# A decoder layer whose compression weights move to buffers of their own, in halves, with the instruction order planned anew

## The chip, the cores and the metric

The kernel runs on one core of a Trainium2 chip. The metric is device time in microseconds (us) of one execution; lower is better. One execution was also taken by the hardware profiler, and all rows below come from it. The engines are TensorE (PE in the rows; PEld is its weight load), VectorE (DVE), ScalarE (ACT), GpSimd (POOL) and SyncE (SP), which issues most transfers.

## The reference, cut to what matters

One layer on 512 tokens of width 1024. A single projection of the normalised input feeds three groups, whose gated outputs are concatenated and projected back:

```python
xn = _rmsnorm(h, g_in[l])
proj = xn @ w_in[l]
...
# A: sparse attention. Its compressed branch first makes 31 blocks of 32 tokens:
def compress(a, pos_emb, w1, w2):
    chunks = a.reshape(B, S // CMP_STRIDE, CMP_STRIDE, G, Dh)
    blocks = jnp.concatenate([chunks[:, r:r + n_cmp] for r in range(R)], axis=2)
    blocks = blocks + pos_emb[:, None, :]
    flat = blocks.transpose(0, 1, 3, 2, 4).reshape(B, n_cmp, G, CMP_LEN * Dh)
    return jax.nn.silu(flat @ w1) @ w2
kc = compress(k_c, pos_k, w1_k, w2_k)
vc = compress(v_c, pos_v, w1_v, w2_v)
...
# B: a chunked state-space scan; its decay matrix is exp of differences of a running sum
decay_in = jnp.exp(jnp.where(causal, a_cs[..., :, None] - a_cs[..., None, :], -jnp.inf))
y_diag = jnp.einsum('bcgels,bcsgep->bclgep', cb[:, :, :, None] * decay_in, xdt)
...
# C: attention into 256 memory tokens
kv = _rmsnorm(mem, g_mem) @ w_mem_kv
...
h = h + jnp.concatenate([o_a, o_b, o_c], axis=-1) @ w_out[l]
return _rmsnorm(h, g_final)
```

## The kernel before, in words

**Arithmetic.** Most products are made of two-part numbers. A weight chunk of 512 KB lands as 128x1024 floats in a tile `wst`; a copy rounds it to `whi` (on ACT or DVE), and a subtraction makes the rest `wlo` (on DVE or POOL). TensorE then multiplies high by high, high by low and low by high. The function `chunk` (line 488) does this for all weights.

**Buffers.** `wst` has two slots (WS), `whi` and `wlo` have three each (WH). A slot of `wst` is free when copy and subtraction are done; a slot of `whi`/`wlo` is free when TensorE has used it. All weights share them: the 24 tiles of the input projection (`in_wd`, product `pj`, 24 matmuls a chunk), the memory keys and values (`in_wmk`, `in_wmv`, product `pjm`), the value projection (`in_wv`, `pjv`), the compression's first layer (`in_w1k`, `in_w1v`, product `ph`, 8 matmuls a chunk, 4 chunks each for keys and values, line 608), the output projection (`pop`, `po`).

**Order.** Nothing is issued as the code runs. A class `Program` records every operation; `plan` (line 258) then plays all five engines forward with a table of costs (`cost`, line 222) and picks for each free engine the ready operation with the lowest number plus a hand-given offset (`BIAS`, and `LEAN` where two engines can do it). That is why every instruction has line 373 in the profile: rows are told apart by tile names. The stages are recorded in the order of the string `ORDER` (line 40): `z0`, `z1` the gate of the scan with the input's norm, `x0` to `x7` the scan's inputs (a convolution in `cacc`, its result `xst` or `bct`, transposed through `pxs`), `m0`, `m1` the memory's norm (`mf`, then `mh`, `ml`), `ki`, `vi` the compression's inputs (`cin`, `ft`, `fs`), `k`, `v` one chunk of the compression each, `mk`, `mv` memory keys and values, `s` one piece of the scan. Behind them come the attention, woven with the remaining projections, and the output projection.

**The scan's decay matrix `R`** (line 1127), one per chunk of 128 tokens, is filled by two transfers: a mask (`R<-in_mt`, on SP's queue), onto which POOL's queue adds the rows of the running sum (`R<-a_rows`). ACT then takes 8 exponentials, DVE multiplies by `pcb`, and TensorE uses it in 8 products `py`.

**Fillers.** TensorE starts with WARM products of zeros (`wps<-idle`) and has SPARE further ones (`wps<-xh`) after the transposes of the input (line 452).

**Tiles the change reuses.** `qst` (5 slots of 128x512) holds the scaled queries (line 720) and `pr` (4 slots) the attention's probabilities (line 797).

Of the kernel before, what the change touches and what calls it, by code (L numbers as in the profile page):

```python
# [42 lines left out]
WA, WX = 53.73, 123.88  # L43
BA, BS, BO = -31, 81, -25
BIAS = {("R", "activation"): 348, ("R", "dma_start"): -287, ("R", "tensor_tensor"): -67, ("a", "dma_start"): 21,
        ("ang", "tensor_copy"): -41, ("at", "activation"): 43, ("bct", "scalar_tensor_tensor"): -71,
        ("btok", "activation"): -227, ("cacc", "scalar_tensor_tensor"): 31, ("cin", "activation"): -1,
        ("cwh", "tensor_scalar"): 45, ("den", "activation"): 129, ("den", "reciprocal"): -233, ("den", "tensor_tensor"): 40,
        ("dout", "activation"): -81, ("dout", "tensor_tensor"): 228, ("dt", "scalar_tensor_tensor"): -45,
        ("dtd", "tensor_tensor"): -48, ("dtr", "tensor_copy"): -10, ("dw", "reciprocal"): 92,  # L50
        ("dw", "scalar_tensor_tensor"): 60, ("dw", "tensor_scalar"): -4, ("dw", "tensor_tensor"): -100,
        ("ea", "activation"): 50, ("eal", "activation"): 94, ("fs", "activation"): 60, ("ft", "tensor_tensor"): 52,
        ("gat", "scalar_tensor_tensor"): 205, ("gin", "dma_start"): -4, ("gps", "matmul"): 83, ("grow", "dma_start"): 2,
        ("gssd", "tensor_scalar"): -2, ("gxt", "scalar_tensor_tensor"): -13, ("idle", "memset"): -100,
        ("kc", "activation"): -112, ("kc", "tensor_tensor"): -52, ("kcs", "memset"): -96, ("kcs", "tensor_copy"): 30,
        ("kcs", "tensor_tensor"): -22, ("kk", "tensor_scalar"): -171, ("km", "activation"): -112, ("km", "tensor_tensor"): -8,
        ("kst0", "activation"): 4, ("kst0", "tensor_tensor"): -124, ("kst1", "tensor_tensor"): -50,
        ("ksw", "stream_shuffle"): 112, ("ksw", "tensor_tensor"): 30, ("lastb", "tensor_copy"): -257,
        ("mf", "tensor_tensor"): -100, ("mh", "activation"): 45, ("mhalf", "activation"): 5, ("mhalf", "memset"): -1,
        ("mhalf", "tensor_scalar"): -100, ("ml", "tensor_tensor"): 124, ("mt", "activation"): -32, ("mt", "dma_start"): 30,  # L60
        ("nacs", "tensor_scalar"): 8, ("o2", "activation"): -208, ("o2", "tensor_tensor"): -98,
        ("oa", "scalar_tensor_tensor"): -68, ("ob", "tensor_tensor"): 57, ("oh", "activation"): 40,
        ("oph", "activation"): 164, ("opl", "tensor_tensor"): 30, ("ot", "activation"): -44, ("pact", "transpose"): -410,
        ("pc", "activation"): 162, ("pc", "tensor_tensor"): 15, ("pcb", "matmul"): -114, ("pcs", "memset"): 243,
        ("pcs", "tensor_tensor"): -10, ("pcs_", "matmul"): -471, ("pjm", "matmul"): -11, ("pjv", "matmul"): -32,
        ("pjz", "matmul"): 105, ("pk", "matmul"): 20, ("po", "matmul"): 44, ("po2", "matmul"): 56, ("po3", "matmul"): 23,
        ("pop", "matmul"): 120, ("posi", "dma_start"): 25, ("pr", "activation"): -30, ("prev", "activation"): 30,
        ("prm", "dma_start"): 165, ("pt", "transpose"): 2, ("pth", "activation"): 405, ("ptl", "tensor_tensor"): 160,
        ("pturn", "transpose"): 96, ("pv", "matmul"): -51, ("pxs", "transpose"): 38, ("py", "matmul"): 234,
        ("py2", "matmul"): -213, ("pyt", "transpose"): 64, ("qr", "tensor_tensor"): -199, ("qst", "activation"): -34,  # L70
        ("qst", "scalar_tensor_tensor"): 429, ("rb", "matmul"): -12, ("rc", "tensor_scalar"): -200,
# [6 lines left out]
        ("vcs", "memset"): -100, ("vm", "activation"): 69, ("vm", "tensor_tensor"): 10, ("vst", "activation"): 30,  # L78
        ("vst", "tensor_tensor"): -15, ("whi", "activation"): 364, ("wlo", "tensor_tensor"): -4, ("wps", "matmul"): -83,
        ("wst", "dma_start"): -15, ("wst0", "dma_start"): -273, ("x", "scalar_tensor_tensor"): 224, ("x", "tensor_tensor"): 8,  # L80
        ("xdd", "tensor_tensor"): -95, ("xdt", "tensor_tensor"): -93, ("xh", "activation"): 96, ("xl", "tensor_tensor"): 150,
        ("xn", "activation"): 136, ("xnm", "reciprocal"): 156, ("xnm", "tensor_reduce"): -287, ("xnm", "tensor_scalar"): -8,
        ("xo", "matmul"): -230, ("xp", "tensor_tensor"): -15, ("xpt", "transpose"): -906, ("xqh", "activation"): 57,
        ("xql", "tensor_tensor"): 79, ("xs", "matmul"): -97, ("xst", "scalar_tensor_tensor"): 48,
        ("xstok", "activation"): -24, ("y", "tensor_tensor"): -192, ("yn", "tensor_scalar"): 85,
        ("yo", "tensor_tensor"): -204, ("z2", "scalar_tensor_tensor"): -64}
# [1387 lines left out]
```

## Time and profile before

| | us |
|---|---|
| three executions | 426.02, 427.02, 431.97 |
| median | 427.02 |
| profiled execution, whole | 426.92 |
| its span, first to last instruction | 425.1 |
| TensorE busy | 407.9 (96%) |
| VectorE busy | 327.4 (77%) |
| ScalarE busy | 217.3 (51%) |
| GpSimd busy | 185.9 (44%) |

Busy time counts a matmul from start to end; matmuls overlap, so two that follow each other without a wait start 0.23 us apart and last 0.4 us each. A wait shorter than that overlap doesn't show as idle time. In a timeline row, the bracket gives the idle time of the engine just before the row and what ended it.

### The profile page before, as it was taken

The numbers are of one execution on the slowest core, as the hardware profiler recorded it, in microseconds if no ns is written. First come the engines' busy times: TensorE is split into PE (matmuls) and PEld (weight loads), VectorE is DVE, ScalarE is ACT, GpSimd is POOL, SyncE is SP. The second block draws the span as 40 slices with busy tenths as digits, with TensorE's granted clock in tenths as the row PEclk, the third lists the DMA queues.
The fourth block names the chain that finished last, engine by engine and source line by source line (L and its number), as shares of the span: only waits on it lengthen the run. The fifth ranks groups of instructions, "written<-read, shape, count | busy, mean of one in ns | idle before, by whom it ended". The sixth has DMA issues, their size and how long they took to land.

```text
span 425.1 us, 6477 instructions
## 1 busy us (share of the span) xinstructions
PE 407.9 (96%) x2319; PEld 349.3 (82%) x2319; DVE 327.4 (77%) x678; ACT 217.3 (51%) x508; POOL 185.9 (44%) x127
## 2 busy tenths in 40 slices
PE   7999999979899999999999999999999999999992
PEld 4998899869788989988888878888787888788871
DVE  4879886687468769787978898897889878767665
ACT  5632355725385336525747366484667674270035
POOL 2552033457734948345553333323256282423142
PEclk9999999989999999999999999999999999999998
DMA  8954318222954534332120211141115103303105
GB/s 289 368 171 153 108 54 194 102 82 98 252 169 146 172 110 126 109 140 99 50 69 32 100 42 59 49 150 49 52 50 199 49 2 99 99 2 99 51 1 197
DMA packets 19572, 47.19 MB, mean 111 GB/s; under 512 B 1586, under 2 KB 8402, under 8 KB 19540
## 3 DMA queue, kind: packets, MB, share of 16 engines
q1 hardware_dynamic: 18816, 44.48, 31.3%
q0 software_dynamic: 576, 2.10, 2.7%
q8 instruction: 18, 0.29, 0.3%
q10 hardware_dynamic: 148, 0.20, 0.1%
q14 instruction: 14, 0.11, 0.1%
HBM read 44.66 MB, written 2.11 MB: 110 GB/s over the span
## 4 chain that ended last, share of the span: by engine, by line
PE 77%; ACT 6%; DVE 6%; DMA 6%; issue 2%; POOL 1%; SPq 0%; POOLq 0%; DVEq 0%; ACTq 0%
PE pj L373 31%; PE pop L373 9%; PE po L373 8%; PE sc L373 5%; PE pjz L373 4%; PE pt L373 4%; PE pjv L373 3%; PE pjm L373 3%; DMA R<-a_rows 2%; DMA wst<-in_wd 2%; PE xs L373 1%; DMA x<-in_x 1%; ACT whi L373 1%; PE xo L373 1%; PE py L373 1%
## 5 line engine op out<-in xcount | busy, mean ns | idle before, releaser
L373 POOL TENSOR_TENSOR wlo<-wst,whi 128x1024 fp32r<-128x1024 f32 (+1 forms) x32 | 76.3, 2389 | 106.0 <-ACT whi L373 60.8
L373 PE MATMUL pj<-xh,whi 128*128 128x512 f32 x224 | 90.7, 405 | 0.0
L373 PE MATMUL pj<-xh,wlo 128*128 128x512 f32 x224 | 90.0, 402 | 0.0
L373 PE MATMUL pj<-xl,whi 128*128 128x512 f32 x224 | 89.1, 398 | 0.0
L373 ACT ACTIVATE whi<-wst 128x1024 fp32r<-128x1024 f32 (+3 forms) x44 | 45.4, 1032 | 38.5 <-PE pj L373 8.6
L373 DVE TENSOR_TENSOR wlo<-wst,whi 128x1024 fp32r<-128x1024 f32 (+3 forms) x32 | 41.9, 1310 | 12.0 <-ACT whi L373 8.8
L373 PEld LDWEIGHTS pj<-xl,whi 128*128 128x128 f32 x224 | 42.6, 190 | 8.3
L373 PEld LDWEIGHTS pj<-xh,wlo 128*128 128x128 f32 x224 | 42.6, 190 | 7.5
L373 PEld LDWEIGHTS pj<-xh,whi 128*128 128x128 f32 x224 | 42.4, 189 | 7.4
L373 ACT ACTIVATE pr<-sc,nm 128x256 f32<-128x256 f32 (+3 forms) x64 | 33.1, 524 | 28.3 <-PE pt L373 16.5
L373 DVE CUSTOM_DVE_ANT_0 sc<-sc,cst 128x256 f32<-128x256 f32 (+3 forms) x64 | 30.9, 495 | 4.3 <-PE sc L373 4.0
L373 DVE TENSOR_TENSOR ptl<-pt,pth 128x512 fp32r<-128x512 f32 x40 | 27.0, 683 | 1.5 <-DVE pth L373 0.5
L373 PE MATMUL sc<-kst,qst 128*128 128x512 f32 (+2 forms) x96 | 27.4, 365 | 0.4 <-ACT pr L373 0.3
L373 PE MATMUL pt<-cst,pr 128*128 128x128 f32 x160 | 27.6, 273 | 0.0
L373 DVE CAST pth<-pt 128x512 fp32r<-128x512 f32 x30 | 20.3, 687 | 7.4 <-PE pt L373 6.9
L373 PE MATMUL pop<-whi,oph 128*128 128x512 f32 x64 | 25.8, 402 | 0.0
L373 PE MATMUL pop<-wlo,oph 128*128 128x512 f32 x64 | 25.4, 399 | 0.0
L373 PE MATMUL pop<-whi,opl 128*128 128x512 f32 x64 | 25.2, 396 | 0.0
L373 PEld LDWEIGHTS pt<-cst,pr 128*128 128x128 f32 x160 | 20.0, 140 | 3.8 <-issue 0.5
L373 PE MATMUL po<-pth,vst 128*128 128x256 f32 x80 | 22.4, 290 | 0.0
L373 PE MATMUL po<-ptl,vst 128*128 128x256 f32 x80 | 21.7, 287 | 0.0
L373 PEld LDWEIGHTS sc<-kst,qst 128*128 128x128 f32 x96 | 16.4, 188 | 4.5 <-ACT pr L373 1.9
(286 smaller groups left out, 995.2 us busy)
## 6 DMA issues: line engine op xcount, KB each, us to landing
wst<-in_wd SPq DMA_DIRECT2D x28, 512.0 KB, 3.3
x<-in_x SPq DMA_DIRECT2D x8, 512.0 KB, 5.1
R<-in_mt SPq DMA_DIRECT2D x4, 512.0 KB, 5.3
R<-a_rows POOLq DMA_DIRECT2D x4, 512.0 KB, 7.9
wst<-in_w1k SPq DMA_DIRECT2D x4, 512.0 KB, 3.6
wst<-in_wmk SPq DMA_DIRECT2D x4, 512.0 KB, 6.4
wst<-in_w1v SPq DMA_DIRECT2D x4, 512.0 KB, 3.5
wst<-in_wmv SPq DMA_DIRECT2D x4, 512.0 KB, 3.7
```

Source lines behind the costliest of these rows:

```text
L373: o["ins"] = getattr(self.engines[o["eng"]].engine, o["fn"])(*o["args"], **o["kw"])
```

## The change

The compression's chunks no longer go through `chunk`, but through `own_chunk`: `wst` stays, the two parts lie in halves of 512 columns in slots of `qst` and `pr`. Each chunk then has two copies and two subtractions of half the width. The matmuls are the same. The planner's costs change for three kinds of operation, WARM goes from 10 to 11, SPARE from 8 to 2, and ORDER, BIAS, LEAN and the weights of the two woven streams are new numbers.

```diff
-ORDER = """z0 x0 x2 x3 x1 rope z1 x4 m0 x6 dt x5 m1 x7 s ki k s mk0 s s k s mk1 k s mk2 k mk3 k vi s v s mv0 s v
-    s s q0 s s v ks v s val s mv1 kw v"""
-WARM, SPARE = 10, 8
+ORDER = """z0 x0 x2 x3 rope x1 z1 x4 x6 x5 m0 dt x7 s m1 ki s s k mk0 k s s mk1 k s mk2 k mk3 s s k vi v mv0 s s
+    s q0 s v s v s val v s ks kw mv1 v"""
+WARM, SPARE = 11, 2
...
             if ins[0].dtype == F32R:
-                return max(109.5, 0.4167 * n + 13.5), 158.0
+                return max(109.5, 0.44 * n + 5.5), 158.0
...
+    def own_chunk(src):
+
+        st = wp.tile([P, WMAX], F32, name="wst", tag="wst", bufs=WS)
+        SY.dma_start(st, src)
+        parts = []
+        for a in (0, S):
+            hi = kp.tile([P, S], F32R, name="chi", tag="qst", bufs=QB)
+            lo = kp.tile([P, S], F32R, name="clo", tag="pr", bufs=PB)
+            X.copy(hi, st[:, a:a + S])
+            X.tensor_tensor(lo, st[:, a:a + S], f(hi), op=OP.subtract)
+            parts.append((hi, lo))
+        return parts
...
         for c in range(4):
-            hi, lo = chunk(A[wname][c], D)
-            hi = hi.rearrange("p (j c) -> p j c", j=4)
-            lo = lo.rearrange("p (j c) -> p j c", j=4)
+            parts = own_chunk(A[wname][c])
             for jj in range(4):
                 st = fs[:, 4 * c + jj].rearrange("p a b -> p (a b)")
-                for w in (hi, lo):
-                    T.matmul(ph[:124], lhsT=st, rhs=w[:, jj], start=n == 0, stop=n == 31)
+                for w in parts[jj // 2]:
+                    T.matmul(ph[:124], lhsT=st, rhs=w[:, jj % 2 * 256:jj % 2 * 256 + 256], start=n == 0, stop=n == 31)
```

**SP's queue, from the last input projections of the scan to the first value chunk.** Before:

```order
L373 DMA wst<-in_wd 128x1024 x2
L373 DMA wst<-in_w1k 128x1024
L373 DMA wst<-in_wmk 128x1024
L373 DMA wst<-in_w1k 128x1024
L373 DMA wst<-in_wmk 128x1024
L373 DMA wst<-in_w1k 128x1024
L373 DMA R<-in_mt 128x8x128 x2
L373 DMA wst<-in_wmk 128x1024
L373 DMA wst<-in_w1k 128x1024
L373 DMA wst<-in_wmk 128x1024
L373 DMA wst<-in_wd 128x1024
L373 DMA wst<-in_w1v 128x1024
```

The same place now:

```order
L379 DMA wst<-in_w1k 128x1024
L379 DMA wst<-in_wmk 128x1024
L379 DMA wst<-in_w1k 128x1024
L379 DMA wst<-in_wmk 128x1024
L379 DMA wst<-in_w1k 128x1024
L379 DMA wst<-in_wmk 128x1024
L379 DMA wst<-in_w1k 128x1024
L379 DMA R<-in_mt 128x8x128
L379 DMA wst<-in_wmk 128x1024
L379 DMA wst<-in_wd 128x1024
L379 DMA R<-in_mt 128x8x128
L379 DMA wst<-in_w1v 128x1024
```

The two masks of the decay matrices stood together ahead of the third `in_wmk`; now they stand apart, the first behind the last `in_w1k` and the second behind the `in_wd` of `vi`.

**DVE, between the results of x6 (first `bct` row) and x5 (last one).** Before:

```order
L373 SCALAR_TENSOR_TENSOR bct<-th_200,cacc 128x512
L373 TENSOR_TENSOR mf<-mf,rb 128x4x128 x2
L373 CAST mh<-mf 128x4x128
L373 SCALAR_TENSOR_TENSOR cacc<-pj,cwh,cacc 128x509
L373 SCALAR_TENSOR_TENSOR cacc<-pj,cwh,cacc 128x510
L373 SCALAR_TENSOR_TENSOR cacc<-pj,cwh,cacc 128x511
L373 TENSOR_TENSOR ml<-mf,mh 128x4x128
L373 SCALAR_TENSOR_TENSOR bct<-th_223,cacc 128x512
```

The same place now:

```order
L379 SCALAR_TENSOR_TENSOR bct<-th_192,cacc 128x512
L379 SCALAR_TENSOR_TENSOR cacc<-pj,cwh,cacc 128x509
L379 SCALAR_TENSOR_TENSOR cacc<-pj,cwh,cacc 128x510
L379 SCALAR_TENSOR_TENSOR cacc<-pj,cwh,cacc 128x511
L379 SCALAR_TENSOR_TENSOR bct<-th_198,cacc 128x512
```

The four operations of `m1` on `mf`, `mh` and `ml` are gone from between them; they now stand 18 rows earlier, ahead of the last three gates of `z1`.

**TensorE, the first products `py` of the scan's third chunk.** Before, they stood inside the compression's last key chunk (`ph` with `whi_293`):

```order
L373 MATMUL pjm_291<-ml_190,whi_289 128x256
L373 MATMUL ph_249<-whi_293,fs_245 124x256
L373 MATMUL py_343<-xdt_276,R_274 128x64 x4
L373 MATMUL ph_249<-wlo_294,fs_245 124x256
L373 MATMUL ph_249<-whi_293,fs_245 124x256
```

Now they stand one matmul into `vi` (`pj_326`):

```order
L379 MATMUL pjm_306<-ml_203,whi_304 128x256
L379 MATMUL pj_326<-xh_77,whi_324 128x512
L379 MATMUL py_350<-xdt_280,R_278 128x64
L379 MATMUL py_350<-xdt_280,R_278 128x64
L379 MATMUL pj_326<-xh_77,wlo_325 128x512
L379 MATMUL pj_326<-xl_79,whi_324 128x512
```

The products moved behind the compression's last key chunk and the whole last memory-key tile (`pjm_306`), and two of them, instead of four, come first.

## Rows read from the trace of the kernel before

**Rows 1.** Windows: us from:to, length, busy (instructions) of PE, PEld, DVE, ACT, POOL; PEclk, DMA share, GB/s.

```profile
28.00:80.00 52.00, 52.00 (x288) 45.00 (x287) 41.26 (x78) 24.05 (x50) 15.04 (x9) 1.00 0.43 127
...
88.00:92.00 4.00, 1.71 (x8) 1.35 (x8) 3.77 (x7) 1.79 (x3) 1.02 (x1) 0.88 0.27 105
...
92.00:98.00 6.00, 6.00 (x29) 5.02 (x28) 3.21 (x5) 1.45 (x4) 2.38 (x3) 0.80 0.30 87
...
111.00:116.00 5.00, 3.29 (x16) 2.58 (x15) 2.31 (x3) 1.54 (x2) 4.04 (x5) 0.89 0.94 222
...
116.00:122.00 6.00, 5.20 (x35) 5.02 (x35) 2.96 (x5) 5.22 (x14) 1.54 (x2) 0.80 0.55 148
...
122.00:160.00 38.00, 37.79 (x237) 33.69 (x235) 28.00 (x43) 17.56 (x34) 22.22 (x16) 1.00 0.46 149
...
190.00:395.00 205.00, 203.78 (x1119) 171.32 (x1118) 168.69 (x413) 115.83 (x303) 85.27 (x51) 1.00 0.21 70
```

**Rows 2.** Waits of TensorE: us in total, times, longest.

```profile
PE pxs L373 <- DVE bct L373: 2.3, 1, 2.3
...
PE pjm L373 <- ACT whi L373: 2.0, 2, 1.6
...
PE py L373 <- DVE R L373: 0.8, 1, 0.8
```

**Rows 3.** Timeline of DVE and POOL from 76 us: start, length; the last row is from the groups.

```profile
84.08 2.54 DVE L373 CAST mh<-mf 128x512 fp32r<-128x512 f32 x1
...
86.54 2.30 DVE L373 SCALAR_TENSOR_TENSOR cacc<-pj,cwh,cacc 128x509 f32<-128x509 f32 x3
...
89.60 0.69 DVE L373 SCALAR_TENSOR_TENSOR bct<-th,cacc 128x512 f32<-128x512 f32 x1 [0.16 <-ACT th L373]
...
83.93 2.40 POOL L373 TENSOR_TENSOR wlo<-wst,whi 128x1024 fp32r<-128x1024 f32 x1 [3.61 <-ACT whi L373]
...
L373 DVE CAST whi<-wst 128x1024 fp32r<-128x1024 f32 x19 | 13.1, 691 | 5.0 <-PE pj L373 2.9 <-issue 0.8 <-PE pop L373 0.7
```

**Rows 4.** Timeline of SP's queue and of ACT, 103 to 117 us.

```profile
103.33 2.17 SPq L373 DMA_DIRECT2D R<-in_mt  x2
...
105.59 0.92 SPq L373 DMA_DIRECT2D wst<-in_wmk  x1
...
112.10 1.06 ACT L373 ACTIVATE whi<-wst 128x1024 fp32r<-128x1024 f32 x1 [4.18 <-DMA wst<-in_wmk]
...
116.78 0.99 ACT L373 ACTIVATE R<-R,nacs 128x128 f32<-128x128 f32 x3 [3.14 <-DMA R<-a_rows]
```

**Rows 5.** The page's part 6: transfers, KB each, median us from issue to landing.

```profile
R<-a_rows POOLq DMA_DIRECT2D x4, 512.0 KB, 7.9
...
wst<-in_w1k SPq DMA_DIRECT2D x4, 512.0 KB, 3.6
...
wst<-in_wmk SPq DMA_DIRECT2D x4, 512.0 KB, 6.4
```

**Rows 6.** Groups by form: count, busy us, mean ns; the idle time before them.

```profile
L373 ACT ACTIVATE whi<-wst 128x1024 fp32r<-128x1024 f32 x39 | 41.2, 1057 | 36.7 <-DMA wst<-in_wd 8.2 <-PE pj L373 7.1 <-issue 6.3
...
L373 ACT ACTIVATE fs<-ft 128x496 fp32r<-128x496 f32 x4 | 2.5, 620 | 0.8 <-POOL ft L373 0.8
...
L373 POOL TENSOR_TENSOR wlo<-wst,whi 128x1024 fp32r<-128x1024 f32 x30 | 72.6, 2422 | 105.8 <-ACT whi L373 60.6 <-DVE whi L373 21.4 <-issue 20.1
...
L373 POOL TENSOR_TENSOR opl<-ox,oph 128x512 fp32r<-128x512 f32 x4 | 5.1, 1297 | 6.8 <-ACT oph L373 6.8
```

**Rows 7.** The chain that ended last: start, length, what (count).

```profile
119.99 1.08 PE py L373 x8
...
124.14 2.84 PE pjm L373 x23
```

**Rows 8.** Timeline of TensorE: the fillers of the first 30 us.

```profile
11.11 1.98 PE L373 MATMUL wps<-xh,idle 128*128 128x512 f32 x5
...
27.75 0.63 PE L373 MATMUL wps<-xh,idle 128*128 128x512 f32 x2
```

More of the change, by code (lines that the diff above doesn't have):

```diff
@@ L37 @@
 SB, TB, JB = 2, 2, 3
-ORDER = """z0 x0 x2 x3 x1 rope z1 x4 m0 x6 dt x5 m1 x7 s ki k s mk0 s s k s mk1 k s mk2 k mk3 k vi s v s mv0 s v
-    s s q0 s s v ks v s val s mv1 kw v"""
-WARM, SPARE = 10, 8
[L43 to L71, printed above, removed]
[6 rows of a table removed]
[L78 to L86, printed above, removed]
@@ new lines @@
+WARM, SPARE = 11, 2
+WA, WX = 56.42, 111.49
+BA, BS, BO = 66, 88, -100
+BIAS = {("R", "activation"): -15, ("R", "dma_start"): -893, ("R", "tensor_tensor"): 46, ("a", "dma_start"): 38,
+        ("ang", "scalar_tensor_tensor"): -56, ("at", "activation"): 79, ("bct", "scalar_tensor_tensor"): -53,
+        ("btok", "activation"): -10, ("cacc", "activation"): -20, ("cacc", "scalar_tensor_tensor"): -60,
+        ("chi", "activation"): -65, ("clo", "tensor_tensor"): -174, ("cst", "dma_start"): 25, ("cwh", "tensor_scalar"): 56,
+        ("dec", "activation"): -68, ("den", "activation"): 13, ("den", "reciprocal"): 58, ("den", "tensor_tensor"): 139,
+        ("dout", "activation"): 2, ("dout", "tensor_tensor"): 74, ("dt", "scalar_tensor_tensor"): -8,
+        ("dtd", "tensor_tensor"): -62, ("dtr", "tensor_copy"): -100, ("dw", "reciprocal"): 8,
+        ("dw", "scalar_tensor_tensor"): -48, ("dw", "tensor_tensor"): 16, ("ea", "activation"): -221,
+        ("eal", "activation"): 90, ("fs", "activation"): 69, ("fs", "tensor_tensor"): -191, ("ft", "tensor_tensor"): 86,
+        ("gat", "scalar_tensor_tensor"): -160, ("gate", "activation"): 6, ("gate", "tensor_scalar"): 331,
+        ("gin", "dma_start"): -60, ("gps", "matmul"): -36, ("gssd", "tensor_scalar"): 116,
+        ("gxt", "scalar_tensor_tensor"): -154, ("hs", "activation"): 2, ("ht", "scalar_tensor_tensor"): 13,
+        ("idle", "memset"): 120, ("kc", "tensor_tensor"): -86, ("kcs", "memset"): 38, ("kcs", "tensor_copy"): 274,
+        ("kcs", "tensor_tensor"): 83, ("kk", "tensor_scalar"): -120, ("km", "activation"): -10, ("kst0", "activation"): -2,
+        ("kst0", "tensor_tensor"): 8, ("kst1", "activation"): -2, ("kst1", "tensor_tensor"): 85,
+        ("ksw", "stream_shuffle"): 34, ("ksw", "tensor_tensor"): 118, ("lastb", "tensor_copy"): 80, ("mf", "dma_start"): -512,
+        ("mf", "tensor_tensor"): -28, ("mh", "activation"): -8, ("mhalf", "activation"): 164, ("mhalf", "memset"): 8,
+        ("mhalf", "tensor_scalar"): -173, ("ml", "tensor_tensor"): 21, ("mt", "activation"): 395,
+        ("nacs", "tensor_scalar"): -71, ("o2", "activation"): -290, ("o2", "tensor_tensor"): -15,
+        ("oa", "scalar_tensor_tensor"): -67, ("ob", "tensor_tensor"): 70, ("oh", "activation"): -98,
+        ("ol", "tensor_tensor"): -120, ("oph", "activation"): 156, ("opl", "tensor_tensor"): 21, ("ot", "activation"): 219,
+        ("out", "dma_start"): 26, ("ox", "scalar_tensor_tensor"): -165, ("pc", "activation"): 39, ("pc", "tensor_tensor"): 66,
+        ("pcb", "matmul"): -301, ("pcs", "activation"): -75, ("pcs", "memset"): 198, ("pcs", "tensor_tensor"): 83,
+        ("pcs_", "matmul"): 8, ("ph", "matmul"): -14, ("pht", "matmul"): 227, ("pj", "matmul"): -14, ("pjm", "matmul"): -16,
+        ("pjv", "matmul"): 12, ("pjz", "matmul"): 361, ("pk", "matmul"): 290, ("po2", "matmul"): 51, ("po3", "matmul"): -154,
+        ("pop", "matmul"): 72, ("posi", "dma_start"): -43, ("pr", "activation"): -229, ("pr", "tensor_tensor"): -98,
+        ("prev", "activation"): 15, ("prev", "tensor_tensor"): -34, ("prm", "dma_start"): 39, ("pst", "matmul"): 342,
+        ("ptc", "transpose"): -242, ("pth", "activation"): -32, ("ptl", "tensor_tensor"): -12, ("pturn", "transpose"): 32,
+        ("pv", "matmul"): -40, ("pxs", "transpose"): 86, ("py", "matmul"): -10, ("py2", "matmul"): -14,
+        ("pyt", "transpose"): 60, ("qr", "tensor_tensor"): -150, ("qst", "activation"): -49,
+        ("qst", "scalar_tensor_tensor"): 38, ("rb", "matmul"): -327, ("rc", "activation"): 160, ("rc", "tensor_scalar"): 241,
[6 rows of a table added]
+        ("vcs", "memset"): 157, ("vcs", "tensor_copy"): -24, ("vcs", "tensor_tensor"): 263, ("vm", "activation"): -2,
+        ("vm", "tensor_tensor"): 100, ("vst", "activation"): -108, ("vst", "tensor_tensor"): -6, ("whi", "activation"): 29,
+        ("wlo", "tensor_tensor"): -160, ("wst", "dma_start"): 5, ("wst0", "dma_start"): -129, ("x", "activation"): 8,
+        ("x", "dma_start"): 30, ("x", "scalar_tensor_tensor"): 224, ("x", "tensor_scalar"): 87, ("x", "tensor_tensor"): 110,
+        ("xdd", "tensor_tensor"): -369, ("xdt", "tensor_tensor"): 34, ("xh", "activation"): -113,
+        ("xn", "scalar_tensor_tensor"): 198, ("xnm", "reciprocal"): -66, ("xnm", "tensor_reduce"): 97,
+        ("xnm", "tensor_scalar"): -250, ("xo", "matmul"): 19, ("xp", "activation"): 100, ("xpt", "transpose"): -656,
+        ("xqh", "activation"): -29, ("xql", "tensor_tensor"): -200, ("xs", "matmul"): -281,
+        ("xst", "scalar_tensor_tensor"): -56, ("xstok", "activation"): 90, ("y", "tensor_tensor"): -305,
+        ("yn", "tensor_scalar"): -500, ("yo", "tensor_tensor"): -12}
@@ new lines @@
+LEAN = {("chi", "ACT"): 100, ("clo", "POOL"): -360, ("fs", "ACT"): 220, ("fs", "POOL"): -100, ("ft", "DVE"): -310,
+        ("km", "ACT"): -100, ("kst0", "ACT"): 250, ("kst0", "DVE"): 70, ("kst0", "POOL"): -90, ("kst1", "DVE"): 40,
+        ("kst1", "POOL"): -150, ("mf", "DVE"): -50, ("mf", "POOL"): 200, ("ml", "POOL"): -70, ("o2", "ACT"): 180,
+        ("o2", "DVE"): 980, ("oh", "ACT"): 200, ("oh", "DVE"): -90, ("ol", "POOL"): 200, ("oph", "DVE"): -60,
+        ("opl", "DVE"): -280, ("opl", "POOL"): 60, ("pcs", "ACT"): 110, ("pcs", "DVE"): -120, ("pr", "DVE"): -220,
+        ("pr", "POOL"): -60, ("pth", "ACT"): -90, ("pth", "DVE"): -60, ("qr", "DVE"): 190, ("sw", "DVE"): 70,
+        ("sw", "POOL"): 250, ("vm", "ACT"): -100, ("vm", "DVE"): 330, ("vst", "ACT"): -40, ("vst", "DVE"): 140,
+        ("whi", "ACT"): -90, ("whi", "DVE"): -230, ("wlo", "DVE"): -200, ("wlo", "POOL"): 120, ("x", "ACT"): 60,
+        ("x", "DVE"): -40, ("xh", "ACT"): -30, ("xh", "DVE"): 60, ("xn", "DVE"): 10, ("xp", "DVE"): 80, ("xp", "POOL"): -60,
+        ("xqh", "ACT"): 50, ("xqh", "DVE"): -220}
```

12 lines of the change are left out of this document (3 added, 9 removed), and 15 rows, old and new, of tables (BIAS, LEAN).

## The prediction

> **What bounds the kernel now.** I read the windows first, because they show in which stretch TensorE is not at work. From 28 to 80 us it is busy without a break, from 122 to 160 us it is idle for 0.21 us of 38, and over the 205 us of the attention for 1.22 us [rows 1]. So nearly all of the time is matmul work that the change leaves alone (the matmuls are the same but for five fillers), and a gain has to come from the stretch between 80 and 122 us, from the head, or from the tail. The reader should see in the four windows of that stretch both idle time and a lower clock: PEclk 0.88, 0.80, 0.89 and 0.80 instead of 1.00.
>
> The list of TensorE's waits then names what is missing: `pxs` waits 2.3 us for a `bct` of DVE, `pjm` 2.0 us in two waits for a `whi` of ACT, `py` 0.8 us for an `R` of DVE; together 5.1 us [rows 2]. After the two long ones the granted clock falls from 2.4 to 1.2 GHz for a while. The missing clock, window by window, is 4 x 0.12 + 6 x 0.20 + 5 x 0.11 + 6 x 0.20 = 3.4 us of full-speed work [rows 1]. It is an upper figure, since part of the low clock falls on idle time. The stretch thus loses about 8.5 us.
>
> The sum is made against the profiled execution, 426.9 us (span 425.1 and 1.8 around it); the median of the runs is 427.0, so one number serves for both.
>
> **The change part by part.**
>
> *The wait for `bct`, 2.3 us and its half-speed part.* DVE's cast `mh` took 2.54 us, while the cast of a twice as wide `whi` takes 0.69 on average; POOL's subtraction ran from 83.93 to 86.33 beside it [rows 3]. Behind it stood the convolution of x5, whose `bct` ended at 90.29. The new order takes `m1` off this place, 18 rows of DVE ahead. What is late next: the chain from the first `cacc` of DVE to the end of `bct` took 86.54 to 90.29, 3.75 us [rows 3], with one ACT step before it some 4.5 us. The new order has the 24 matmuls of x7 in front of that `pxs`, 24 x 0.23 = 5.5 us, so some 1 us is to spare. I count the wait as gone: its 2.3 us, and the clock loss of the first two windows, 0.5 + 1.2. Ends: -4.0, and 0 if DVE is late there for another reason.
>
> The Trainium skill (SBUF — State Buffer, section Who interferes with whom) says that VectorE and GpSimd share one pair of ports, which an instruction holds until it ends, so that a cast on VectorE blocks fully when GpSimd came first. The row of `mh` agrees: its end, 86.62 us, lies 0.3 us behind the end of POOL's subtraction. By that rule the change has a price, since eight half-width subtractions now stand on POOL. It would also shorten the longest block, from 2.4 to 1.3 us; the sum is the same by the rule and by the row, as TensorE no longer waits behind that cast.
>
> *The waits for `whi`, 2.0 us, and their half-speed part.* The third `in_wmk` was issued at 105.59, behind two masks `R` at 103.33, and ACT could copy it only at 112.10, having waited 4.18 us for the landing [rows 4]. Its median to landing is 6.4 us where `in_w1k` has 3.6 [rows 5]. It was issued that late because compression and memory chunks drew on the same three `whi` slots. With slots of their own, two compression chunks can be split during x5, x7 and `ki`, and the `in_wmk` chunks move up with them. The queue now also has one mask in place of two, behind the last `in_w1k`. I count 2.0 us and the clock loss of the last two windows, 0.55 + 1.2, as gone. Ends: -3.7, and 0 if the transfers stay that slow.
>
> *The wait for `R`, 0.8 us*, goes as such; what takes its place is below.
>
> *The halves.* A chunk's copy on ACT goes from 1.06 us to about 2 x 0.62, its subtraction on POOL from 2.42 to 2 x 1.30 [rows 6]. Eight chunks cost ACT some 1.5 us and POOL up to 1.5 us more. Both lie beside TensorE; ACT is busy 17.56 of 38 us behind this stretch [rows 1], which hides them. Without that cover the first matmuls of a chunk would wait for 0.2 us at most, as the first half is ready earlier than a whole one.
>
> *The fillers.* WARM is one more and SPARE six fewer. Of the eight spare ones three stood between matmuls that were ready: two take 0.63 us with the overlap of the last, that is 0.23 each, so 0.7 us goes. The other five took 1.98 us in a wait for the first weights [rows 8]; leaving them out gains nothing in itself. But SP now issues the first large weight chunk ahead of the second block of the input, and its copy need not stand behind that block's square on ACT. I bound that by 0 and by the 1.98 us, and take half, 1.0.
>
> *The new waits.* The mask of the third `R` reuses a slot, so it waits for the first chunk's last `py`, then for POOL's add, the exponentials on ACT and the multiplication on DVE. Before, this took from 103.33 [rows 4] to the `py` at 119.99 [rows 7], 16.7 us. Between the same two points TensorE now has 64 `pjm` and 16 `ph` (0.123 us each by 2.84 / 23), and some 16 small products (0.27 each, by 1.08 for the eight records of four products) and one `pj`: 9.8 + 4.3 + 0.2 = 14.3 us [rows 7]. That leaves 2.4 us of waiting. On the other side one mask, not two, is under way at once. Ends: 0, and 2.4 with another 2.4 when POOL's add stands behind a subtraction [rows 6] and 1.7 for the clock, 6.5. I take 1.5, nearer to the row. Behind this wait on ACT, in order, stand the copies for the memory values, and `vi` needs a `wlo` that is now POOL's, 2.42 us [rows 6]. For both together I take 1.0, with 0 and 4 as ends (a transfer at 6.4 instead of 3.6 [rows 5], and a subtraction's extra second).
>
> *Attention and tail.* The order is another one, the work is not; DVE loses some casts to ACT. With 1.22 us idle in 205 [rows 1] there is little to win. I take 0, with -1 and +3.
>
> The sum: -8.5 (waits and clock) - 0.7 - 1.0 (fillers, head) + 1.5 + 1.0 (new waits) = -7.7. 426.9 - 7.7 = 419.2, so 419.
>
> **The rivals.**
>
> *No new waits.* The mask lands early, since it is alone. Then -8.5 - 1.7 = -10.2, and with a head at its better end and the shorter waits that the rows show as busy time some 11 us: 416. For it: the row with 16.7 us had two masks on the queue. Against it: DMA was at 0.94 of its capacity in 111 to 116 us [rows 1], and the same bytes must pass.
>
> *The change does not do what it says.* The slots were not what held the weights: the two `wst` slots and the transfers pace the stretch, and DVE's chain is late again. Then only the fillers, the head and some 2 us remain: 423.5. For it: both kinds of chunk still pass through the same two `wst` slots. Against it: from 122 us on, chunk follows chunk and TensorE hardly waits [rows 1].
>
> *Slower.* Moving the chunks up packs masks, adds and weights together, and every weight transfer takes the 6.4 us of the `in_wmk` rows rather than 3.6 [rows 5] from `mk3` to the value projection. That is twelve chunks on two slots, 12 x 2.8 / 2 = 17 us of waiting: 426.9 - 7.7 + 17 = 436. It decides against the change from the point where the twelve lose 7.7 us, 1.3 us more for each landing than 3.6. Against it: the masks no longer stand on the queue as a pair, and the DMA share behind this stretch was 0.46 [rows 1].
>
> **How the numbers follow.** The forecast, 419 and what lies between 417 and 421.5, gets 0.45; no new waits (below 417) 0.28; not as said (421.5 to 426) 0.20; slower 0.07. Two per cent of 427 is 8.5 us, about what a measurement of this kernel can tell from no change. Faster by over 2% means below 418.4: all of the first rival and a third of the forecast, 0.43. Slower by over 2% needs most of the slower rival's price, 0.04. Within 2% is the rest, 0.53. The range for 8 in 10 takes in the first rival's 416 with the better ends of its terms and most of the second one: 413.5 to 425.5.
>
> **What would show it.** Right: between 80 and 122 us TensorE's windows at PEclk 1.00 or nearly, no wait of `pxs` for DVE above 0.5 us, `in_wmk` landing in about 4 us, and a wait of 1 to 3 us of the third chunk's `py` or of `vi` at its first matmuls. The five steps are each wrong if their wait stands there still. The forecast as a whole is wrong if the attention, 205 us before, is more than 3 us longer or shorter, since no term was given to it, or if a single new wait exceeds 4 us.

## The result, and the profile after

The changed kernel takes 421.54 us (median of four runs, 420.02 to 422.38) where the kernel before takes 427.44: ratio 0.9855, 95% interval 0.9815 to 0.9894. That is 5.9 us, 1.4%. The forecast was 419, with 413.5 to 425.5 as its range. The profiled execution took 420.02 us (span 418.3), 6.9 less than the one of before. Two executions in a slower state, one of b_mask below (460.40 us, at a granted clock of 0.84) and one of the kernel before (432.09 us), are left out of the times and ratios of the experiments.

The windows of the kernel after, in the stretches of [rows 1], columns as there:

```profile
28.00:80.00 52.00, 51.51 (x284) 44.38 (x283) 42.99 (x79) 25.80 (x52) 21.09 (x12) 1.00 0.45 130
...
88.00:92.00 4.00, 4.00 (x20) 3.23 (x19) 3.23 (x5) 1.38 (x3) 1.28 (x1) 1.00 0.69 228
92.00:98.00 6.00, 6.00 (x47) 5.73 (x46) 5.00 (x8) 3.53 (x9) 6.00 (x5) 1.00 0.30 88
...
111.00:116.00 5.00, 4.73 (x33) 4.28 (x33) 2.92 (x4) 3.75 (x10) 3.29 (x3) 1.00 1.05 278
116.00:122.00 6.00, 6.00 (x33) 5.10 (x31) 5.17 (x12) 2.60 (x6) 4.86 (x5) 1.00 0.86 186
122.00:160.00 38.00, 35.63 (x254) 33.72 (x253) 28.93 (x41) 18.75 (x42) 28.81 (x22) 1.00 0.40 116
...
190.00:395.00 205.00, 204.75 (x1125) 170.94 (x1124) 167.51 (x403) 123.82 (x316) 77.64 (x48) 1.00 0.21 68
```

The reader should see two things. From 88 to 122 us TensorE is idle for 0.27 us in all and its clock is at 1.00 throughout, where [rows 1] had 0.80 to 0.89 in four windows. And from 122 to 160 us it is idle for 2.4 us where it was idle for 0.21: that is new. TensorE's waits name it, in place of [rows 2]:

```profile
PE pjv L379 <- ACT whi L379: 1.6, 1, 1.6
...
PE pjm L379 <- ACT whi L379: 0.8, 1, 0.8
PE pj L379 <- DVE z L379: 0.3, 1, 0.3
```

No `pxs` waits for a `bct` any more, and no `py` for an `R`. The `bct` that ended at 90.29 [rows 3] now ends at 86.70, as DVE's timeline says:

```profile
85.44 1.26 DVE L379 SCALAR_TENSOR_TENSOR bct<-th,cacc 128x512 f32<-128x512 f32 x1 [0.76 <-ACT th L379]
```

The transfers (part 6 of the page) and the halves (groups by form) answer to [rows 5] and [rows 6]:

```profile
R<-a_rows POOLq DMA_DIRECT2D x4, 512.0 KB, 6.8
wst<-in_w1k SPq DMA_DIRECT2D x4, 512.0 KB, 3.6
wst<-in_wmk SPq DMA_DIRECT2D x4, 512.0 KB, 4.5
```

```profile
L379 POOL TENSOR_TENSOR clo<-wst,chi 128x512 fp32r<-128x512 f32 x8 | 12.3, 1542 | 5.9 <-ACT chi L379 4.7 <-DVE chi L379 1.1 <-PE ph L379 0.2
L379 DVE TENSOR_TENSOR clo<-wst,chi 128x512 fp32r<-128x512 f32 x8 | 9.6, 1204 | 0.7 <-ACT chi L379 0.7
L379 ACT ACTIVATE chi<-wst 128x512 fp32r<-128x512 f32 x15 | 8.8, 624 | 10.3 <-DMA wst<-in_w1k 5.3 <-DMA wst<-in_w1v 4.0 <-PE ph L379 1.0
```

**Where the time went.** Idle time hides waits shorter than the overlap of two matmuls, so I took for each matmul the time from its start to the next one's start, less the step at which matmuls of its kind follow each other without a wait (0.23 us for 512 columns, 0.12 for 256, 0.11 for a transpose). The remainder, lost time at TensorE, is summed over all rows of PE. The stretches are cut at the same amount of finished work, so that they hold the same matmuls, but for order and fillers, in each kernel; they are named by their times in the kernel before.

| lost at TensorE, us | 0–30 | 30–80 | 80–122 | 122–160 | behind | all |
|---|---|---|---|---|---|---|
| before | 5.3 | 0.1 | 9.6 | 0.9 | 6.5 | 22.5 |
| after | 6.8 | 0.5 | 0.7 | 2.9 | 5.5 | 16.3 |

That is 6.1 us, and five fillers fewer are 1.1 more. TensorE ends at 409.80 instead of 417.03; the tail behind it is 0.4 us longer.

### The profile page after: what moved, and what is told of

Its sections match the earlier page's. It is cut to its first block, busy times and chain, and to the rows that moved or that the text cites. A ratio compares the mean times of both kernels' runs of the same rounds, so it can differ in the third digit from the quotient of the medians.

```text
span 418.3 us, 6475 instructions
## 1 busy us (share of the span) xinstructions
PE 403.9 (97%) x2314; PEld 346.4 (83%) x2314; DVE 324.0 (77%) x662; ACT 229.9 (55%) x530; POOL 194.6 (47%) x137
## 4 chain that ended last, share of the span: by engine, by line
PE 86%; POOL 4%; DMA 4%; ACT 3%; DVE 1%; issue 1%; SPq 0%; POOLq 0%; DVEq 0%; ACTq 0%
PE pj L379 34%; PE po L379 11%; PE pop L379 11%; PE pjz L379 5%; PE sc L379 5%; PE pt L379 4%; PE pjm L379 4%; PE pjv L379 3%; DMA R<-a_rows 2%; PE xs L379 1%; PE xo L379 1%; DMA x<-in_x 1%; PE ph L379 1%; PE pturn L379 1%; POOL wlo L379 1%
## 5 line engine op out<-in xcount | busy, mean ns | idle before, releaser
L379 POOL TENSOR_TENSOR wlo<-wst,whi 128x1024 fp32r<-128x1024 f32 (+2 forms) x29 | 69.4, 2396 | 98.4 <-ACT whi L379 44.3
L379 PE MATMUL pj<-xh,wlo 128*128 128x512 f32 x224 | 89.0, 397 | 0.0
L379 ACT ACTIVATE whi<-wst 128x1024 fp32r<-128x1024 f32 (+3 forms) x42 | 43.2, 1031 | 43.4 <-PE pop L379 11.9
L379 ACT ACTIVATE pr<-sc,nm 128x128 f32<-128x128 f32 (+3 forms) x64 | 33.1, 524 | 18.9 <-DVE nm L379 9.6
L379 DVE TENSOR_TENSOR wlo<-wst,whi 128x1024 fp32r<-128x1024 f32 (+3 forms) x27 | 38.7, 1435 | 6.0 <-ACT whi L379 5.6
L379 DVE CUSTOM_DVE_ANT_0 sc<-sc,cst 128x128 f32<-128x128 f32 (+3 forms) x64 | 31.4, 497 | 3.0 <-PE sc L379 2.3
L379 PE MATMUL pt<-cst,pr 128*128 128x128 f32 x160 | 30.4, 274 | 0.0
L379 PE MATMUL sc<-kst,qst 128*128 128x512 f32 (+2 forms) x96 | 29.9, 364 | 0.0
L379 PE MATMUL po<-pth,vst 128*128 128x256 f32 x80 | 22.5, 289 | 0.0
L379 DVE CAST pth<-pt 128x512 fp32r<-128x512 f32 x20 | 13.7, 689 | 9.9 <-PE pt L379 9.2
L379 ACT ACTIVATE pth<-pt 128x512 fp32r<-128x512 f32 x20 | 11.8, 596 | 16.9 <-PE pt L379 16.7
```

The costliest lines, as they stand in the source:

```text
L379: o["ins"] = getattr(self.engines[o["eng"]].engine, o["fn"])(*o["args"], **o["kw"])
```

## The experiments

All kernels below were run beside the kernel before, whose medians were 426.8 to 427.7. Where one says "order word for word", the planner runs as it did, and only the listed operations are taken out of its order and put elsewhere, or on another engine, right before issuing:

```diff
         end = self.plan()
-        for _, n in self.order:
+        for n, e in WAYS.items():
+            o = self.ops[n]
+            o["eng"], o["fn"], o["args"], o["kw"] = o["ways"][e][:4]
+        seq = [n for _, n in self.order]
+        for n, m in MOVES:
+            seq.remove(n)
+            seq.insert(seq.index(m), n)
+        for n in seq:
```

My theory S: the slots are the gain. The rival O: the order is, and could have been had without slots.

| kernel | time in us, ratio [interval] | lost 0–30 | 80–122 | 122–160 | behind |
|---|---|---|---|---|---|
| b_own | 426.45, 0.995 [0.990, 1.000] | 4.8 | 7.4 | 1.4 | 6.4 |
| b_m1 | 423.25, 0.990 [0.978, 1.002] | 4.9 | 5.3 | 1.9 | 6.5 |
| b_mask | 428.73, 1.003 [0.999, 1.008] | 5.2 | 10.4 | 1.7 | 6.4 |
| b_m1_mask | 426.99, 1.000 [0.995, 1.004] | 6.8 | 8.3 | 0.9 | 6.4 |
| b_own_m1 | 425.44, 0.997 [0.993, 1.000] | 4.8 | 6.9 | 1.6 | 6.4 |
| e_order_only | 430.13, 1.007 [1.004, 1.011] | 6.1 | 8.2 | 2.2 | 8.3 |
| e_slots_only | 432.06, 1.011 [1.005, 1.018] | 7.8 | 3.9 | 7.6 | 8.1 |
| a_m1back | 422.78, 0.988 [0.984, 0.992] | 7.2 | 2.1 | 5.5 | 5.4 |
| a_xfirst | 422.47, 0.987 [0.983, 0.990] | 5.8 | 0.8 | 2.5 | 5.4 |
| a_waits | 420.38, 0.983 [0.980, 0.985] | 7.3 | 1.0 | 4.2 | 5.5 |
| a_best | 419.24, 0.981 [0.978, 0.983] | 7.1 | 1.1 | 2.0 | 5.3 |
| a_best2 | 417.08, 0.977 [0.972, 0.982] | 6.6 | 0.9 | 2.3 | 5.3 |

The losses, in us and in the stretches of the table above, are those of the one profiled execution. The time is the median of the runs, 4 to 10 of each kernel; the ratio is worked out from the single runs on both sides, so it isn't exactly the quotient of two medians. An interval that reaches 1 means that no difference is shown.

**The slots alone (b_own).** The order of before word for word; the planner still counts three shared slots, the parts lie elsewhere, and the second half is copied and subtracted right behind the first, on the same engine:

```diff
-            hi, lo = chunk(A[wname][c], D)
+            parts = own_chunk(A[wname][c])
```

> The kernel before with its order of instructions word for word; only the compression's weight parts lie in slots of their own, in halves, the two halves copied (and subtracted) one right after the other. Theory S (the slots are the gain): the chunk copied at 98.73 us no longer waits for a slot of whi, what hangs on it moves up by 1 to 2 us, both waits for whi (2.0 us) and the low clock behind them (1.75) shrink; the wait for bct (2.3 and 1.7) stays: 423 to 424.5 us. Theory O (the order is the gain, the slots only allow it): both waits stand as before, and the halves cost nothing that TensorE sees: 426 to 427.5 us.

Measured 0.6 us of gain by the medians, 2.2 us less loss between 80 and 122 us. It is not what I had expected of S: the wait for `bct` fell from 2.3 to 0.8 us (with 0.5 more at a `pcb`), and the clock behind it stayed at 1.00 from 88 to 98 us, because POOL's subtraction is in halves there and DVE's cast `mh` was held up for a shorter time (below). The copy of 98.73 us only moved along with what stands ahead of it. ACT's rows of before and of b_own (start, length):

```profile
97.14 1.56 ACT L373 ACTIVATE cin<-pj 64x256 f32<-64x256 f32 x4 [3.29 <-PE pj L373]
98.73 1.06 ACT L373 ACTIVATE whi<-wst 128x1024 fp32r<-128x1024 f32 x1
```

```profile
94.27 1.57 ACT L407 ACTIVATE cin<-pj 64x256 f32<-64x256 f32 x4 [1.95 <-PE pj L407]
95.87 0.63 ACT L407 ACTIVATE whi<-wst 128x512 fp32r<-128x512 f32 x1
```

The copy stands behind `cin` in the order, and with a slot of its own it still stands there. Here a free slot was worth nothing to an order that doesn't use it; what b_own gained came from the halves.

**The place of m1 alone (b_m1), the mask alone (b_mask), both (b_m1_mask).** On DVE and SP of the kernel before, in shared slots (the matmul `rb` that `mf` needs moves up too):

```diff
 DVE  bct<-th_185,cacc
+DVE  mf<-mf,rb  (x2), mh<-mf, ml<-mf,mh
 DVE  wlo<-wst,whi
...
 DVE  bct<-th_200,cacc
-DVE  mf<-mf,rb  (x2), mh<-mf
 DVE  cacc<-pj,cwh,cacc  (x3)
-DVE  ml<-mf,mh
```

```diff
 SP   R_274<-in_mt
-SP   R_337<-in_mt
 SP   wst_288<-in_wmk
+SP   R_337<-in_mt
 SP   wst_292<-in_w1k
```

> The kernel before with one thing moved: the four DVE operations of m1 (mf twice, mh, ml) and the matmul rb they need go ahead of the subtraction that DVE began at 74.96 us, into idle time of DVE. Shared slots stay. If the place of m1 was the cause of the wait for bct, the 2.3 us and the 1.7 us of low clock behind it go: 423 us. If DVE is late there for another reason (POOL's subtraction holding it up at the next operation), the wait stays at over 1.5 us: 426 to 427 us.

> The kernel before with one thing moved: on SP's queue the second of the two masks R goes behind the third in_wmk instead of ahead of it. Shared slots stay. If the masks ahead of it made that in_wmk land late, it lands in under 5 us instead of 6.4, the longest wait for whi falls from 1.6 us to under 0.5 and the clock stays up: 423.5 us. If the slots (its late issue at 105.59) or the capacity of the transfers are the cause, the wait stays over 1 us or turns up at the mask's products py: 426 to 427.5 us.

> Both moves together, shared slots. Theory O: the two gains add to some 7 us, as much as the whole change: 419.5 to 421 us. Theory S: only m1's part comes, 423 us, since the memory keys still wait for slots.

m1's move took 4.3 us of loss away, and the time came out at 423.25, though the interval of four runs still holds 1. The move of the mask gained nothing: `in_wmk` landed in 6.2 us by the median, not in under 5. TensorE's waits of b_mask show where a gain could have gone:

```profile
PE ph L382 <- ACT whi L382: 1.7, 1, 1.7
PE pjm L382 <- ACT whi L382: 1.5, 2, 1.2
```

`pjm` waits 1.2 us instead of 1.6 [rows 2], and the next chunk, whose transfer now stands behind the mask, makes `ph` wait 1.7. With both moves together the wait of that `ph` is 3.4 us, and b_m1's gain is gone. So rival O, as I had it, is out: these two moves of the order alone do not add to the change. Nor is it what I expected of S, which left b_m1's 423.

**Slots and m1, nothing else (b_own_m1).** The edits of b_own and b_m1 together.

> The kernel before with its order, the slots apart (as in b_own) and m1 moved (as in b_m1), and nothing else. The two alone took 2.2 and 4.3 us off TensorE's waiting between 80 and 122 us. If they add, 6.5 of the change's 8.9 us are slots and m1, and the order of the weight transfers has the rest: 420 to 421 us. If the slots' gain was part of the same wait for bct, they don't add: 422.5 to 423.5 us. If the order is needed to use the slots, the waits for whi stand there still at over 1 us each.

They don't add: 6.9 us are lost between 80 and 122, more than b_m1's 5.3. The third case of the expectation came about in the main: `ph` waits 2.2 us for a `whi`, `pjm` 0.9 at the longest. The order is needed to use the slots.

**The new order in shared slots (e_order_only), the new slots under the old tables (e_slots_only).** In both the planner plans anew.

```diff
-            parts = own_chunk(A[wname][c])
+            hi, lo = chunk(A[wname][c], D)
```

```diff
-            hi, lo = chunk(A[wname][c], D)
+            parts = own_chunk(A[wname][c])
...
+BIAS = {("chi", "activation"): 364, ("clo", "tensor_tensor"): -4,
+LEAN = {("chi", "ACT"): -270, ("chi", "DVE"): 200, ("clo", "DVE"): 30, ("clo", "POOL"): 480,
```

> The changed kernel with all its tables, but the compression's chunks go through the shared slots again, whole; the order is planned from these tables. Its m1 stands early, as in the changed kernel, but its weights' queue has the two masks as a pair ahead of the third in_wmk again. Theory S (slots are needed for the later part): the wait for bct is gone and the waits for whi stay, so it lies where b_m1 lies, 423 to 425 us. Theory O: within 1 us of the changed kernel, 421.5 us.

> The kernel before with all its tables and costs (the halves get the offsets of whi and wlo), and the compression's chunks through the new function; the order is planned from these tables. Its queue takes all four w1k and all four wmk chunks ahead of the masks. Theory S: the waits for whi go; m1 stands where it stood, with the cast mh on ACT, so the wait for bct is shorter than 2.3 us: 420 to 422.5 us. Theory O: the new tables are needed, and new waits take the place of the old: 425 to 429 us.

Both are slower than the kernel before, by 0.7% and 1.1%. Without the slots the planner puts the two masks ahead of the third `in_wmk` again, and `ph` waits 3.5 us, `pjm` 1.4:

```profile
PE ph L379 <- ACT whi L379: 3.5, 1, 3.5
```

Without the new tables the slots do clear 80 to 122 us (3.9, of which 1.7 is the wait for `bct`), but 7.6 us are lost from 122 to 160. So neither the new tables without the slots nor the slots without the new tables gave a faster kernel, and both together gave 5.9 us. That is as far as it is shown: b_m1 may have gained 3.8 us by an order alone, and as the planner plans anew, e_order_only doesn't have the order of the changed kernel. No run has slots of their own without halves, and none tells the new costs of the planner apart from its other tables. What order and slots do together shows in two windows, 80 to 98 and 98 to 116 us, of the kernel before, the changed one, b_own_m1 and e_order_only:

```profile
80.00:98.00 18.00, 15.71 (x71) 12.59 (x71) 14.15 (x18) 6.12 (x11) 7.57 (x6) 0.91 0.28 88
98.00:116.00 18.00, 15.92 (x122) 15.01 (x121) 11.19 (x14) 7.65 (x13) 15.57 (x13) 0.97 0.66 186
```

```profile
80.00:98.00 18.00, 18.00 (x104) 15.57 (x103) 14.53 (x19) 9.70 (x18) 13.09 (x9) 1.00 0.45 138
98.00:116.00 18.00, 17.73 (x143) 17.18 (x143) 10.13 (x13) 8.64 (x19) 15.31 (x13) 1.00 0.74 200
```

```profile
80.00:98.00 18.00, 17.71 (x104) 15.26 (x102) 14.99 (x18) 10.52 (x19) 12.62 (x10) 1.00 0.30 88
98.00:116.00 18.00, 13.50 (x99) 12.34 (x99) 9.36 (x14) 6.71 (x18) 11.32 (x10) 1.00 0.90 234
```

```profile
80.00:98.00 18.00, 18.00 (x107) 15.61 (x106) 13.62 (x18) 8.55 (x16) 7.47 (x5) 1.00 0.19 64
98.00:116.00 18.00, 12.93 (x89) 11.69 (x89) 11.88 (x12) 8.41 (x20) 14.40 (x12) 0.88 0.92 233
```

The last two columns are the DMA share and GB/s. Of these four only the changed kernel moves its weights early: 138 GB/s from 80 to 98 us, where the others move 64 to 88; b_own_m1 and e_order_only then run at a share of 0.90 and 0.92 while TensorE waits. Of all kernels in shared slots none moves more than 114 GB/s there (b_m1_mask); e_slots_only, which has the slots and an order planned with them, moves 141:

```profile
80.00:98.00 18.00, 15.92 (x76) 12.74 (x75) 13.71 (x18) 11.34 (x22) 12.93 (x9) 1.00 0.46 141
```

The changed kernel can, because the second `in_w1k` chunk is copied at 85.31 instead of 98.73. Copy and subtractions empty its `wst` slot, and the third `in_w1k` is issued at 88.47 instead of 101.78. The copy in the changed kernel, then that in e_order_only:

```profile
85.31 1.14 ACT L379 ACTIVATE chi<-wst 128x512 fp32r<-128x512 f32 x2
```

```profile
94.64 1.06 ACT L379 ACTIVATE whi<-wst 128x1024 fp32r<-128x1024 f32 x1
```

The products `ph` of the first two chunks start 14 us later, at 99.22. Until then the copy needs a place to lie in; that, as I read it, is the slot's part. The row of e_order_only fits: there, with three shared slots, the same chunk was issued at 84.33 and copied behind `cin`. No run makes the early copy in shared slots, so the reading isn't shown. It would explain b_own_m1 and b_m1_mask too: with `bct` out of the way TensorE is sooner at products whose weights come no sooner.

**m1 put back in the changed kernel (a_m1back).** The reverse of b_m1's edit, in the order of the changed kernel.

> The changed kernel with its order, only m1 (mf twice and mh on DVE, ml and ACT's and POOL's part behind them) put back between the results of x6 and x5, the place that it had before. If the place of m1 made the wait for bct, the bct that ended at 86.70 us ends 3 us later or more, beside POOL's subtraction from 83.74, and pxs waits 2 to 3 us for it, with some low clock behind: 424 to 426 us. If the slots gave slack there (the rival), under 0.5 us: 421 to 422 us.

By the trace the rival is nearer: `bct` ends 1.4 us later, at 88.09, and `pxs` waits 0.17 us for it. The median is 1.2 us above the changed kernel's, between the two cases, with overlapping intervals. In the new order the 24 matmuls of x7 stand ahead of that `pxs`, and they just covered m1 as it ran here. But the cast `mh` came ahead of POOL's subtraction in this run and took 0.43 us, not the 2.54 of the kernel before (rows below). Had it come second, `bct` would have ended some 2 us later still, an estimate from these two rows, and `pxs` would have waited. Its profiled execution lost 1.4 us more between 80 and 122 and 2.6 more from 122 to 160, in the waits for `whi` there; I can't tell how much of that belongs to the edit.

**The head (a_xfirst), the two new waits (a_waits), both (a_best).** The edit on SP's queue is a_xfirst's, the others are a_waits':

```diff
 SP   wst0<-in_wz
-SP   cst, x_71, wst_91, x_71, wst_95, x_94, cst, x_94, mf, prm
+SP   x_71, cst, x_71, wst_91, wst_95, x_94, x_94, cst, prm, mf
...
-DVE  chi_336<-wst
+ACT  chi_336<-wst      (behind chi_334)
+ACT  whi_343<-wst      (ahead of cin_327, x4)
 ACT  cin_327<-pj       (x4)
-ACT  whi_343<-wst
+DVE  wlo_395<-wst,whi  (ahead of qr_362)
-POOL wlo_395<-wst,whi
```

> The changed kernel with its order, only SP's queue in the head as before the change: the first block of the input ahead of the constants, the second ahead of the second weights, the rest behind them. In the changed kernel ACT got its first block at 6.96 us instead of 5.04, and TensorE had done 0.5 us less work by 30 us although it ran five fillers fewer. If that queue is why the head gave nothing, the first matmul of weights starts 1 to 2 us earlier and the time is 420 to 420.7 us. If TensorE's head is set by the copies on ACT and DVE behind it, or varies by itself from execution to execution, no difference outside the interval: 421 to 422 us.

> The changed kernel with three operations on the copies' side placed otherwise: the second half's copy of the first w1v chunk on ACT right behind the first half instead of on DVE behind five others; the copy of the second in_wmv ahead of the four cin on ACT; the subtraction of the first in_wv on DVE instead of on POOL, which freed the slot only at 143.89 us. If these queues made the two waits for whi behind 122 us (0.95 and 1.73 us between matmuls), both fall below 0.3 us: 419 to 419.5 us. If the transfers or the masks' add stand behind, the waits move by less than 0.5 us or turn up at the next chunk: 421 to 422 us.

> Both sets of moves together. If they are independent they add: 418 to 418.5 us, over 2% below the kernel before (ratio 0.979). If a head that ends earlier only makes TensorE wait longer for the weights behind 80 us, as it did in b_own_m1, it lies with a_waits: 419.5 us.

a_xfirst did not change the time. Its first block came earlier, but ACT then waited for weights, which had moved back; here ACT's rows of the changed kernel and of a_xfirst:

```profile
6.96 1.06 ACT L379 ACTIVATE xn<-x 128x1024 f32<-128x1024 f32 x1 [3.90 <-DMA x<-in_x]
...
8.25 0.85 ACT L379 ACTIVATE whi<-wst 128x792 fp32r<-128x792 f32 x1
```

```profile
5.00 1.06 ACT L388 ACTIVATE xn<-x 128x1024 f32<-128x1024 f32 x1 [1.94 <-DMA x<-in_x]
...
8.88 0.86 ACT L388 ACTIVATE whi<-wst 128x792 fp32r<-128x792 f32 x1 [2.50 <-DMA wst<-in_wz]
```

a_waits gained 1.2 us by the medians, with overlapping intervals and less than the expected 2 to 2.5; in its profiled execution, the slowest of its six, a `pjm` still waits 1.2 us for a `whi`. a_best shows what was next in line: its wait of `pjv` for `whi` is gone, and `pjv` waits 1.2 us for DVE's `qr` instead, because I had put the subtraction ahead of it.

```profile
141.79 1.87 DVE L388 TENSOR_TENSOR wlo<-wst,whi 128x840 fp32r<-128x840 f32 x1
143.58 0.68 DVE L388 TENSOR_TENSOR qr<-pj,rc 128x512 f32<-128x512 f32 x1
```

**That wait taken away, and two small ones (a_best2).**

```diff
 DVE  qr_362<-pj,rc
+DVE  wlo_395<-wst,whi  (now behind qr_362)
...
+DVE  z2<-th,pjz        (x2, ahead of the copy whi_194)
 DVE  whi_194<-wst
+ACT  whi_128<-wst      (ahead of mh_202)
 ACT  mh_202<-mf
```

> The kernel of a_best with the one wait that its moves made taken away, and two small ones of the changed kernel: the subtraction of the first in_wv goes on DVE behind qr instead of ahead of it (pjv waited 1.3 us for qr at 142.97), the two gates z that pj waits for at 64.6 us go ahead of a copy whi on DVE (0.44 us), and the copy of the first in_wd on ACT goes ahead of mh (0.36 us). If each wait was that one operation's, they go: 417 to 417.5 us. If something else is next in line, within 0.5 us of a_best, 418.7 to 419.7 us.

417.08 us, as expected, and 4.5 us below the changed kernel by the medians, though the intervals of the ratios still touch; it is the fastest of all. The waits for `qr` and for `z` are gone. The move of `whi_128` was a miss: the first `pj` now waits 0.7 us, and a `py` and a `pjm` as long for an `R` and a `whi`:

```profile
PE pj L388 <- ACT whi L388: 0.7, 1, 0.7
```

## Why the prediction was right, and where it wasn't

**The waits and the clock between 80 and 122 us, -8.5.** Right in size: the loss there fell by 8.9 us, every window is at 1.00, and `in_wmk` lands in 4.5 us (about 4 in the forecast). The reason was given too simply. I wrote that slots of their own let the chunks be split earlier, and this stands; but I counted m1's place as a gain of its own, and in the changed kernel m1's place is worth little as long as the cast `mh` isn't held up (a_m1back), since x7's matmuls cover it. In the kernel before it is worth 4.3 us of loss (b_m1). m1's early place and x7's matmuls ahead of `pxs` are two ways to remove one wait.

**The halves, hidden.** Right: a copy half takes 0.624 us against the 0.62 that I took. The subtraction halves on POOL take 1.54 instead of 1.30, beside DVE; neither shows at TensorE by itself.

**The fillers and the head, -1.7.** This step failed. The five fillers fewer save 1.1 us, and the head loses 1.4 us more (the table's 5.3 and 6.8 are rounded), so that the step gives nothing. I had seen that a weight chunk moved up on SP's queue and overlooked that the constants had moved ahead of the first block of the input, which ACT got at 6.96 us instead of 5.04:

```profile
5.04 1.06 ACT L373 ACTIVATE xn<-x 128x1024 f32<-128x1024 f32 x1 [1.99 <-DMA x<-in_x]
```

Putting it back did not help by the medians (a_xfirst); ACT then waited for weights. How much of the 1.4 us belongs to the change stays open, for kernels with the head of before lost 4.8 to 6.8 us there (b_own and b_m1_mask).

**The new waits, +2.5.** Right in size (2.0 us more between 122 and 160, 0.4 between 30 and 80), wrong in place, so that the size is luck. I had put 1.5 on the third mask's `py`, where nothing waits, and 1.0 on `vi` and the memory values behind it. The chain that ended last, from 112 us, shows that the mechanism came one matrix later:

```profile
113.76 2.00 POOL wlo L379
115.77 0.47 issue
116.25 6.66 DMA R<-a_rows
122.94 0.99 ACT R L379 x3
...
126.81 0.95 ACT whi L379
...
127.80 0.74 PE pjm L379 x4
...
141.50 2.40 POOL wlo L379
143.91 3.71 DMA wst<-in_wv
147.71 0.91 ACT whi L379
148.66 1.44 PE pjv L379 x9
```

POOL's add to the fourth `R` stands behind a subtraction, as my upper bound had it; ACT's exponentials wait for its landing, behind them stands the copy for the memory values, and `pjm` waits 0.8 us. The second wait I had not seen: the subtraction of an `in_wv` chunk is on POOL behind `fs`, `y`, `prev` and others, and its `wst` slot comes free only at 143.91.

**Attention and tail, 0.** Within its bounds: 1.0 us less loss, a tail 0.4 longer.

Summed by these terms: -8.9 + 0.3 + 2.4 - 1.0 + 0.4 is -6.8, which is the difference of the two spans, 425.1 and 418.3, against -7.7 forecast. The failed step, the head, is larger than the whole difference. By the medians 421.54 lies on the border between the forecast and "not as said"; the trace decides between them, and it has the waits gone. "No new waits" fell by the trace as well, but its counter-argument was weak: I had taken a DMA share of 0.94 for the capacity, and from 111 to 116 us the changed kernel moved 278 GB/s where before it was 222. The slower one resembles another kernel: from 98 to 116 us e_order_only has its transfers packed together (0.92) and TensorE waiting.

## What to carry to other kernels

A buffer and an order belong together: in this kernel a slot more was worth what the order made of it, and an order that runs ahead needs somewhere to put what it has prepared. So when both are changed, try each alone as well, before the gain is put down to either. Moving one thing out of TensorE's way often brings it earlier to the next thing that is late (b_mask, b_own_m1, a_best); ask for each removed wait when the weights behind it land.
